# Gated delta rule on one core: GpSimd masks the decay before the rows' scales are known

## The chip, the cores and the metric

The kernel runs on one core of a Trainium2 chip, as one program with one launch. The metric is the device time of an execution in microseconds, the median of three runs. The profile is one execution that the hardware profiler recorded; its times count from the start of its span.

## The reference, cut to what matters

Two blocks run one after the other on 256 frames of width 1024 in float32. The first mixes two branches, a gated delta rule (8 heads of 64) and a sparse attention with an indexer, and then a mixture of experts. The second has a gated linear recurrence, an attention with forgetting and a dense feed-forward part. The change lies in the delta rule of the first block. It works in chunks of 64 frames; what it needs before its scan over the chunks is this (cut):

```python
G = jnp.cumsum(gc, axis=-1)
incl = idx[:, None] >= idx[None, :]
strict = idx[:, None] > idx[None, :]
decay = jnp.exp(jnp.where(incl, G[..., :, None] - G[..., None, :], -jnp.inf))
kk = jnp.einsum("bhnid,bhnjd->bhnij", kc, kc)
a_mat = jnp.where(strict, bc[..., :, None] * kk * decay, 0.0) + jnp.eye(CHUNK)
sol = lax.linalg.triangular_solve(a_mat, rhs, left_side=True, lower=True, unit_diagonal=True)
qk = jnp.einsum("bhnid,bhnjd->bhnij", qc, kc) * decay
k_dec = kc * jnp.exp(G[..., -1:] - G)[..., None]
```

The keys and queries are normalised first, so each row of the products also gets a factor of 1/norm. The decay, 64x64 for each of 8 heads and 4 chunks, is masked once strictly (for the triangular matrix) and once inclusively (for qk).

## The kernel before

Dense products (`tm`, L318, with tokens as rows; `fm`, L359, with features as rows) run in float32 split in two parts: a weight chunk `raw` comes by DMA from SP's queue, ACT rounds it to `whi` (L298), DVE subtracts to get `wlo` (L301), and TensorE adds three products (L333, L334, L335 in `tm`; L374, L375 or L379 to L381 in `fm`). Each of these tiles has four buffers. An accumulator `acc` in PSUM has to be emptied before its next use.

The branches are written as generators and drained piece by piece by `stream`; a scheduler at compile time then fixes the order in which each engine's queue takes its instructions. An engine takes its queue strictly in that order. So an edit in one place can give other orders for some hundreds of instructions on all engines.

The function `delta` (L583) runs, for each half `t` of 128 frames: the squares and norms of the queries and keys (`rk[t]` by the root iterations L179 to L199), the running log decay `R` (L629) and its product L632, the exponential `dec` (L634, ACT), the column `wk` of it (L644) and the scaled keys `kd` (L646, DVE), `br2` (L654), then four GpSimd products of 128x512 that give the masked and scaled decays `dl` and `di` (L658 to L663), and the products of keys and queries (L671, L672), which DVE multiplies with them to `LT` and `QK` (L673, L674). After both halves DVE scales keys and queries (L678, L679). From `LT` then follows, for both halves at once, a chain: `E` (L691 on ACT, L692 on DVE), `F`, `Lr`, `Ti`, fifteen pairs of small DVE instructions (L703, L705) that invert the 16x16 diagonal blocks, then L712 to L717, `DT` (L720) and `DD` (L724, ACT), the TensorE groups L737 with DVE's `X` (L741) between them, and the scan over the chunks (L774 to L803).

Beside it TensorE has the dense products of the same block to do: the third part of the convolution, four column groups `z_group` of the indexer (`zI`, two groups of 292 columns) and of the attention (`zB`, two groups of 384 columns), later the gate product with 512 columns (`sz`), then the wide `fm` products of the mixing gates (L374). The indexer's scores (L926) and the attention's logits (L955) lie between them. For each `z_group` ACT copies the two accumulators to `zI` or `zB` (L820).

Of the kernel before, what the change touches and what calls it, by code (L numbers as in the profile page):

```python
# [14 lines left out]
ALU = mybir.AluOpType  # L15
# [56 lines left out]
def body(ctx, tc, I, out, dbg=None):  # L72
    nc = tc.nc
    V, A, G, T, SY = nc.vector, nc.scalar, nc.gpsimd, nc.tensor, nc.sync
# [11 lines left out]
    def nm(s):  # L86
        cnt[0] += 1
        return f"{s}{cnt[0]}"
# [23 lines left out]
    def b2(shape, dt=F32, n="c"):  # L112
        return sp.tile(shape, dt, tag="b2" + st[0], name=nm(n), bufs=NB2[st[0]])
# [4 lines left out]
    def tiny(shape, dt=F32, n="t"):  # L118
        n_el = int(np.prod(shape[1:]))
        if n_el > 64:  # L120
            return sp.tile(shape, dt, tag="t128", name=nm(n), bufs=4)
        tag, bufs = ("t16", N16) if n_el <= 16 else ("t64", N64)
        return sp.tile(shape, dt, tag=tag + st[0], name=nm(n), bufs=bufs[st[0]])
# [12 lines left out]
    def sm():  # L136
        return pss.tile([128, 512], F32, tag="sm" + st[0], name=nm("sm"), bufs=NSM[st[0]])
# [12 lines left out]
    def C(k):  # L150
        o, n = COFF[k]
        return cst[:, o:o + n]
# [18 lines left out]
    def rsqrt(v, shape):  # L171
        return rsqrts([v], shape)[0]
# [404 lines left out]
    def hv(ap):  # L577

        return ap.rearrange("p (b q) -> p q b", q=2)
# [3 lines left out]
    def delta():  # L583
# [14 lines left out]
        rk, rki, kd, vs = [], [], [], []  # L598
# [3 lines left out]
        for t in range(2):  # L602
            ts_ = slice(t * 128, (t + 1) * 128)
            tk = []
            for src in (qT, kT):
                ps = sm()
                for b in range(4):
                    T.transpose(ps[:, b * 128:(b + 1) * 128], src[:, b, ts_], ident)
                tk.append(ps)
                junk = b2([128, 8, 64], n="sq")  # L610
                A.activation(junk.rearrange("p h d -> p (h d)"), ps, AF.Square)
                ss = tiny([128, 8])
                V.tensor_reduce(ss, junk, axis=AX.X, op=ALU.add)
                if src is qT:
                    oe = tiny([128, 8])
                    V.tensor_scalar(oe, ss, 64 * EPS, 256 * EPS * EPS, op0=ALU.mult, op1=ALU.add)
                    oeps.append(oe)
                else:
                    vv = tiny([128, 8])
                    V.tensor_scalar(vv, ss, 4 * EPS, None, op0=ALU.add)  # L620
                    r = rsqrt(vv, [128, 8])
                    ri = tiny([128, 8])
                    V.scalar_tensor_tensor(ri, vv, 0.5, r, op0=ALU.mult, op1=ALU.mult)
                    rk.append(r)
                    rki.append(ri)
            yield

            R = b2([128, 2, 4, 64], n="R")
            V.tensor_tensor(R, hv(gg[:, t])[:, :, :, None].to_broadcast([128, 2, 4, 64]),  # L629
                            C("inc")[:, None, None].to_broadcast([128, 2, 4, 64]), op=ALU.mult)  # L630
            pe = sm()
            T.matmul(pe, C("v64"), R.rearrange("p q b i -> p (q b i)"), start=True, stop=True)  # L632
            dec = b2([128, 2, 4, 64], n="dec")
            A.activation(dec.rearrange("p q b i -> p (q b i)"), pe, AF.Exp)  # L634
            pg = sm()
            gx = b2([128, 8, 64], n="gx")
            V.tensor_copy(gx, gg[:, t, :, None].to_broadcast([128, 8, 64]))
            for b in range(4):
                T.matmul(pg[:, b * 128:(b + 1) * 128], gx[:, 2 * b:2 * b + 2].rearrange("p h d -> p (h d)"), C("u64"),
                         start=True, stop=True)  # L640
            A.activation(eG[:, :, ts_], pg.rearrange("p (b t) -> p b t", b=4), AF.Exp)

            wk = tiny([128, 2, 4])
            V.tensor_tensor(wk, hv(rk[t]), dec[:, :, :, 63], op=ALU.mult)  # L644
            k_ = b2([128, 2, 4, 64], n="kd")
            V.tensor_tensor(k_, tk[1].rearrange("p (b q d) -> p q b d", q=2, d=64),  # L646
                            wk[:, :, :, None].to_broadcast([128, 2, 4, 64]), op=ALU.mult)
            kd.append(k_)
            yield

            br = tiny([128, 8])
            V.tensor_tensor(br, bet[:, t], rk[t], op=ALU.mult)
            br2 = tiny([128, 8])
            V.tensor_tensor(br2, br, rk[t], op=ALU.mult)  # L654
            oeps[t] = (oeps[t], br)
            dl = b2([128, 2, 4, 64], n="dl")
            di = b2([128, 2, 4, 64], n="di")
            G.tensor_tensor(dl, hv(br2)[:, :, :, None].to_broadcast([128, 2, 4, 64]),  # L658
                            C("str")[:, None, None].to_broadcast([128, 2, 4, 64]), op=ALU.mult)
            G.tensor_tensor(di, hv(rk[t])[:, :, :, None].to_broadcast([128, 2, 4, 64]),  # L660
                            C("inc")[:, None, None].to_broadcast([128, 2, 4, 64]), op=ALU.mult)
            G.tensor_tensor(dl, dl, dec, op=ALU.mult)
            G.tensor_tensor(di, di, dec, op=ALU.mult)  # L663
            for q in range(2):
                pk = sm()
                p4 = pk.rearrange("p (a b i) -> p a b i", a=2, b=4)
                for c in range(2):
                    cs = slice(t * 128 + c * 64, t * 128 + c * 64 + 64)
                    rw = slice(q * 64, q * 64 + 64)
                    for b in range(4):  # L670
                        T.matmul(p4[c * 64:c * 64 + 64, 0, b], kT[rw, b, cs], kT[rw, b, cs], start=True, stop=True)  # L671
                        T.matmul(p4[c * 64:c * 64 + 64, 1, b], kT[rw, b, cs], qT[rw, b, cs], start=True, stop=True)  # L672
                V.tensor_tensor(LT[:, t, q], p4[:, 0], dl[:, q], op=ALU.mult)  # L673
                V.tensor_tensor(QK[:, t, q], p4[:, 1], di[:, q], op=ALU.mult)  # L674
            yield
# [84 lines left out]
        for n in range(4):  # L760
            t, c = divmod(n, 2)
# [46 lines left out]
            yield  # L808

    dl_ = delta()  # L810
    stream("a", dl_)
    conv(2, vT)
# [1005 lines left out]
```

## Time and profile before

| | |
|---|---|
| median of three runs | 876.07 us (874.96 to 876.17) |
| time of the profiled execution | 880.68 us |
| span of the profiled execution | 878.9 us |
| mean granted TensorE clock | 0.981 |
| TensorE busy | 831.4 us, 95% of the span |
| VectorE (DVE) busy | 600.0 us, 68% |
| ScalarE (ACT) busy | 419.0 us, 48% |
| GpSimd (POOL) busy | 60.0 us, 7% |

Busy shares are means over stages with different limits. The profiled execution's own time stands 4.6 us above the median of the runs and 1.8 us above its span, so a time worked out from rows of the trace is on the trace's scale and has to be brought to that of the runs.

### The profile page before, as it was taken

What the parts mean: (1) busy time and instruction counts of PE and PEld (TensorE: products, weight loads), DVE (VectorE), ACT (ScalarE), POOL (GpSimd) and SP (SyncE); (2) the same over time, 40 slices, a digit from 0 to 9 for tenths busy, and PEclk for the clock granted to TensorE, in tenths of its full rate; (3) what the DMA queues carried; (4) which work ended last, traced back from release to release, by engine and by line L of the source; (5) the groups of instructions that cost most, each with busy time, mean ns of one, the idle gap of its engine ahead of it and who ended that gap; (6) DMA issues with size and microseconds to landing.
All of it is one profiled execution on the core that took longest, in us unless ns stands there. A gap on an engine that the chain in (4) does not pass through costs nothing.

```text
span 878.9 us, 14638 instructions
## 1 busy us (share of the span) xinstructions
PE 831.4 (95%) x5565; PEld 696.1 (79%) x5565; DVE 600.0 (68%) x1303; ACT 419.0 (48%) x743; POOL 60.0 (7%) x74
## 2 busy tenths in 40 slices
PE   4998899999998999999797998999999999999997
PEld 4997878788887766655797985889888888888876
DVE  5977996797777342415769789656886666674565
ACT  4754544366554011013664544665566556663443
POOL 5022030000000000000106103000000000000000
PEclk9999999799998999999899999999999999999999
DMA  8732561253678899966362573355665666675641
GB/s 232 205 87 73 173 195 50 66 173 114 221 272 300 293 385 348 385 212 207 130 185 72 141 218 110 91 168 189 211 197 150 188 191 186 180 212 198 193 158 48
DMA packets 107721, 162.81 MB, mean 185 GB/s; under 512 B 7272, under 2 KB 73584, under 8 KB 107648
## 3 DMA queue, kind: packets, MB, share of 16 engines
q1 hardware_dynamic: 107008, 161.71, 57.9%
q8 instruction: 45, 0.74, 0.3%
q0 software_dynamic: 640, 0.13, 0.2%
q14 instruction: 28, 0.23, 0.1%
HBM read 159.71 MB, written 2.11 MB: 184 GB/s over the span
## 4 chain that ended last, share of the span: by engine, by line
PE 43%; DVE 6%; issue 2%; ACT 1%; POOL 0%; DVEq 0%; POOLq 0%; ACTq 0%
PE acc L374 13%; PE acc L375 6%; PE acc L333 5%; PE acc L334 5%; PE acc L335 5%; PE acc L380 1%; PE acc L381 1%; PE acc L379 1%; PE sm L272 1%; DVE wlo L301 1%; PE sm L1662 1%; PE sm L1566 1%; PE sm L1690 1%; DVE ST L1567 0%; PE sm L1682 0%
## 5 line engine op out<-in xcount | busy, mean ns | idle before, releaser
L301 DVE TENSOR_TENSOR wlo<-raw,whi 128x1024 fp32r<-128x1024 f32 (+4 forms) x203 | 241.1, 1190 | 93.3 <-ACT whi L298 90.0
L298 ACT ACTIVATE whi<-raw 128x1024 fp32r<-128x1024 f32 (+4 forms) x203 | 207.0, 1022 | 149.9 <-PE acc L335 53.4
L374 PE MATMUL acc<-hx,whi 128*128 128x512 f32 x608 | 214.1, 403 | 0.9 <-DVE hx L255 0.9
L375 PE MATMUL acc<-hx,wlo 128*128 128x256 f32 x608 | 161.6, 286 | 0.0
L333 PE MATMUL acc<-whi,hx 128*128 128x512 f32 (+4 forms) x376 | 139.6, 371 | 7.3 <-ACT zI L820 3.7
L335 PE MATMUL acc<-whi,hx 128*128 128x512 f32 (+4 forms) x376 | 138.4, 368 | 0.0
L334 PE MATMUL acc<-wlo,hx 128*128 128x512 f32 (+4 forms) x376 | 138.4, 368 | 0.1
L374 PEld LDWEIGHTS acc<-hx,whi 128*128 128x128 f32 x608 | 110.5, 190 | 23.0 <-issue 1.3
L375 PEld LDWEIGHTS acc<-hx,wlo 128*128 128x128 f32 x608 | 115.9, 191 | 8.0 <-issue 0.7
L333 PEld LDWEIGHTS acc<-whi,hx 128*128 128x128 f32 x376 | 71.1, 189 | 18.4 <-ACT zI L820 4.5
L380 PE MATMUL acc<-hx,whi 128*128 128x256 f32 x288 | 81.6, 284 | 1.4 <-DVE hx L258 1.4
L379 PE MATMUL acc<-hx,whi 128*128 128x256 f32 x288 | 81.1, 284 | 1.5 <-ACT hx L257 1.5
L381 PE MATMUL acc<-hx,wlo 128*128 128x256 f32 x288 | 81.9, 285 | 0.0
L335 PEld LDWEIGHTS acc<-whi,hx 128*128 128x128 f32 x376 | 71.1, 189 | 9.8 <-issue 0.5
L334 PEld LDWEIGHTS acc<-wlo,hx 128*128 128x128 f32 x376 | 71.2, 189 | 9.3 <-DVE wlo L301 0.5
L1253 PE MATMUL acc<-we,xg 128*64 128x256 f32 x512 | 64.8, 383 | 0.0
L379 PEld LDWEIGHTS acc<-hx,whi 128*128 128x128 f32 x288 | 54.8, 192 | 2.4 <-ACT hx L257 2.0
L380 PEld LDWEIGHTS acc<-hx,whi 128*128 128x128 f32 x288 | 55.2, 191 | 2.0 <-DVE hx L258 1.8
L381 PEld LDWEIGHTS acc<-hx,wlo 128*128 128x128 f32 x288 | 55.2, 192 | 0.4 <-issue 0.2
L1253 PEld LDWEIGHTS acc<-we,xg 128*64 128x64 f32 x512 | 37.8, 137 | 21.3 <-issue 5.4
L386 DVE TENSOR_TENSOR both<-both,acc 128x256 f32<-128x256 f32 x76 | 31.6, 416 | 20.9 <-ACT both L385 20.0
L385 ACT ACTIVATE both<-acc 128x256 f32<-128x256 f32 x76 | 28.8, 380 | 33.6 <-PE acc L374 33.5
(456 smaller groups left out, 1126.1 us busy)
## 6 DMA issues: line engine op xcount, KB each, us to landing
raw<-in_w_in SPq DMA_DIRECT2D x64, 512.0 KB, 3.8
we<-in_w_exp_gate SPq DMA_DIRECT2D x32, 512.0 KB, 7.6
we<-in_w_exp_up SPq DMA_DIRECT2D x32, 512.0 KB, 7.9
wd<-in_w_exp_down SPq DMA_DIRECT2D x64, 256.0 KB, 6.5
raw<-in_w_ffn_gate SPq DMA_DIRECT2D x22, 512.0 KB, 3.8
raw<-in_w_ffn_up SPq DMA_DIRECT2D x22, 512.0 KB, 3.9
raw<-in_w_ffn_down SPq DMA_DIRECT2D x22, 512.0 KB, 4.4
raw<-in_w_out SPq DMA_DIRECT2D x16, 512.0 KB, 4.3
```

The source lines that it names most:

```text
L298: A.activation(hi[:, :n], raw[:, :n], AF.Copy)
L301: (eng or V).tensor_tensor(lo[:, :n], raw[:, :n], hi[:, :n].bitcast(F32), op=ALU.subtract)
L333: T.matmul(ps[t][:, c], ht.hi(kk, a, b), wh[:, k, c], start=kk == 0, stop=False)
L334: T.matmul(ps[t][:, c], ht.hi(kk, a, b), wl[:, k, c], start=False, stop=False)
L335: T.matmul(ps[t][:, c], ht.lo(kk, a, b), wh[:, k, c], start=False, stop=kk == K - 1)
L374: two = [lambda: T.matmul(ps[f], wh[:, k, c], ht.both(kk), start=kk == 0, stop=kk == K - 1), lambda: T.matmul(ps[f][:, :S], wl[:, k, c], h ...
L375: lambda: T.matmul(ps[f][:, :S], wl[:, k, c], ht.hi(kk), start=False, stop=False)]
L379: T.matmul(ps[f][:, :S], wh[:, k, c], ht.hi(kk), start=kk == 0, stop=False)
L380: T.matmul(ps[f][:, :S], wh[:, k, c], ht.lo(kk), start=False, stop=False)
L381: T.matmul(ps[f][:, :S], wl[:, k, c], ht.hi(kk), start=False, stop=kk == K - 1)
L386: V.tensor_tensor(both, both, ps[f][:, :S], op=ALU.add)
L1253: T.matmul(ph[64 * q:64 * q + 64, i * 256:(i + 1) * 256], xgs[pr // 2][k // 4][:, k % 4, e * 64:(e + 1) * 64], ups[ex][k // 4, i][:, k % 4 ...
```

## The change

For each half, GpSimd now multiplies the decay with the strict mask into `dl` and with the inclusive mask in place (`di` is `dec`'s own tile) right behind the exponential. `wk` reads its column after that (column 63 of the inclusive mask is one in all its rows, so the value is the same). Once the rows' scales are there, one GpSimd product puts `br2` into `dl` and one DVE product puts `rk[t]` into `di`. Line numbers on the left of the diff's second part are not those of the kernel before: L658 to L663 before answer to L637, L639, L661, L662 after, and `wk` is L649 instead of L644.

```diff
             dec = b2([128, 2, 4, 64], n="dec")
             A.activation(dec.rearrange("p q b i -> p (q b i)"), pe, AF.Exp)
+
+            dl = b2([128, 2, 4, 64], n="dl")
+            G.tensor_tensor(dl, dec, C("str")[:, None, None].to_broadcast([128, 2, 4, 64]), op=ALU.mult)
+            di = dec
+            G.tensor_tensor(di, dec, C("inc")[:, None, None].to_broadcast([128, 2, 4, 64]), op=ALU.mult)
             pg = sm()
             gx = b2([128, 8, 64], n="gx")
...
             V.tensor_tensor(br2, br, rk[t], op=ALU.mult)
             oeps[t] = (oeps[t], br)
-            dl = b2([128, 2, 4, 64], n="dl")
-            di = b2([128, 2, 4, 64], n="di")
-            G.tensor_tensor(dl, hv(br2)[:, :, :, None].to_broadcast([128, 2, 4, 64]),
-                            C("str")[:, None, None].to_broadcast([128, 2, 4, 64]), op=ALU.mult)
-            G.tensor_tensor(di, hv(rk[t])[:, :, :, None].to_broadcast([128, 2, 4, 64]),
-                            C("inc")[:, None, None].to_broadcast([128, 2, 4, 64]), op=ALU.mult)
-            G.tensor_tensor(dl, dl, dec, op=ALU.mult)
-            G.tensor_tensor(di, di, dec, op=ALU.mult)
+            G.tensor_tensor(dl, dl, hv(br2)[:, :, :, None].to_broadcast([128, 2, 4, 64]), op=ALU.mult)
+            V.tensor_tensor(di, di, hv(rk[t])[:, :, :, None].to_broadcast([128, 2, 4, 64]), op=ALU.mult)
             for q in range(2):
```

Three places show how the orders move. The first is DVE's queue at the second half (t = 1), from `wk` on. Before:

```order
169 L644 TENSOR_TENSOR t_795<-ry_767,dec_785 128x8
170 L652 TENSOR_TENSOR t_799<-t_588,ry_767 128x8
171 L646 TENSOR_TENSOR kd_797<-sm_752,t_795 128x512
172 L654 TENSOR_TENSOR t_801<-t_799,ry_767 128x8
173 L678 TENSOR_TENSOR qkvT_250<-qkvT_250,eG_634 128x1024
174 L679 TENSOR_TENSOR qkvT_249<-qkvT_249,eG_634 128x1024
175 L673 TENSOR_TENSOR LT_632<-sm_809,dl_803 128x256
176 L674 TENSOR_TENSOR QK_633<-sm_809,di_804 128x256
```

The same place of the changed kernel (`dec_784` is the tile that GpSimd masks in place; `wlo_1605` is the last weight part of the second `zI` group):

```order
168 L649 TENSOR_TENSOR t_797<-ry_766,dec_784 128x8
169 L657 TENSOR_TENSOR t_801<-t_588,ry_766 128x8
170 L651 TENSOR_TENSOR kd_799<-sm_751,t_797 128x512
171 L659 TENSOR_TENSOR t_803<-t_801,ry_766 128x8
172 L662 TENSOR_TENSOR dec_784<-dec_784,ry_766 128x512
173 L677 TENSOR_TENSOR qkvT_250<-qkvT_250,eG_634 128x1024
174 L672 TENSOR_TENSOR LT_632<-sm_807,dl_786 128x256
175 L673 TENSOR_TENSOR QK_633<-sm_807,dec_784 128x256
176 L672 TENSOR_TENSOR LT_632<-sm_826,dl_786 128x256
178 L678 TENSOR_TENSOR qkvT_249<-qkvT_249,eG_634 128x1024
179 L691 SCALAR_TENSOR_TENSOR E_847<-LT_632,cst,E_847 128x16x16 x2
180 L301 TENSOR_TENSOR wlo_1605<-raw_1601,whi_1603 128x584
```

A new 128x512 product (L662) stands in the queue, the second scaling of the queries has moved behind `LT` and `QK`, and `wlo_1605`, which before was taken at row 157, ahead of the root iterations, now stands behind `E`.

The second place is DVE's queue where the weight parts of the second `zB` group are made, within and behind the chain of small instructions. Before (`wlo_1705` is that group's first chunk):

```order
210 L703 TENSOR_TENSOR t_893<-Lr_856,Ti_858 128x48
211 L301 TENSOR_TENSOR wlo_1705<-raw_1701,whi_1703 128x768
212 L705 TENSOR_TENSOR Ti_858<-Ti_858,t_893 128x4x12
213 L301 TENSOR_TENSOR wlo_1723<-raw_1719,whi_1721 128x768
214 L703 TENSOR_TENSOR t_896<-Lr_856,Ti_858 128x39
215 L301 TENSOR_TENSOR wlo_1741<-raw_1737,whi_1739 128x768
```

The changed kernel, where the same first chunk is `wlo_1703`:

```order
226 L716 TENSOR_TENSOR y_909<-Y_907 128x16x16
227 L714 STREAM_TRANSPOSE Y_914<-Z_912 128x512
228 L719 TENSOR_TENSOR DT_904<-y_909,cst 128x1024
229 L716 TENSOR_TENSOR y_916<-Y_914 128x16x16
230 L301 TENSOR_TENSOR wlo_1703<-raw_1699,whi_1701 128x768
231 L572 SCALAR_TENSOR_TENSOR qkvT_251<-ct_1176,cy_1171 128x256
232 L301 TENSOR_TENSOR wlo_1721<-raw_1717,whi_1719 128x768
233 L301 TENSOR_TENSOR wlo_1739<-raw_1735,whi_1737 128x768
```

The chunk has moved from the twelfth pair of the loop to behind the whole chain up to `DT` and `y`.

The third place is TensorE's queue around the first group of L737 (the first use of `DD`). Before, it comes when the second `zB` group is all but done:

```order
582 L335 MATMUL acc_1700<-whi_1757,hx_134 128x384
583 L333 MATMUL acc_1700<-whi_1757,hx_134 128x384
584 L737 MATMUL sm_924<-DD_905,LT_632 64x64 x16
585 L334 MATMUL acc_1700<-wlo_1759,hx_134 128x384
586 L335 MATMUL acc_1700<-whi_1757,hx_134 128x384
587 L333 MATMUL acc_2190<-whi_2194,hx_131 128x512
```

In the changed kernel it comes behind the sixth matmul of that group:

```order
537 L335 MATMUL acc_1622<-whi_1679,hx_134 128x384
538 L333 MATMUL acc_1697<-whi_1701,hx_131 128x384
539 L334 MATMUL acc_1697<-wlo_1703,hx_131 128x384
543 L335 MATMUL acc_1697<-whi_1701,hx_131 128x384
544 L736 MATMUL sm_922<-DD_903,LT_632 64x64 x16
545 L333 MATMUL acc_1698<-whi_1701,hx_131 128x384
```

Forty matmuls of 128x384 thus stand behind L737's first group instead of ahead of it. Later in the queue, between the first L737 and the first wide `fm` matmul (L374), before has 2 of 128x384 and 48 of 128x512 among the small products, all 48 ahead of the last logits (L955). The changed kernel has 42 of 128x384 and 20 of 128x512 there, and the other 28 of 128x512 in one piece between L955 and L374.

## Rows read from the trace of the kernel before

**Rows 1.** The cores' spans and mean granted clock.

```profile
core 0: 878.9 us, clock 0.981
```

**Rows 2.** Windows of 20 us: length, busy time of each engine (instructions), clock, DMA.

```profile
80.00:100.00 20.00, 15.61 (x92) 14.69 (x92) 16.71 (x52) 7.88 (x12) 2.45 (x2) 1.00 0.36 112
100.00:120.00 20.00, 17.67 (x285) 15.06 (x284) 19.90 (x44) 13.79 (x22) 1.97 (x2) 1.00 0.49 143
...
140.00:160.00 20.00, 20.00 (x192) 15.80 (x192) 13.04 (x32) 7.93 (x18) 0.00 (x0) 0.83 0.17 54
160.00:180.00 20.00, 20.00 (x96) 16.70 (x95) 15.52 (x45) 9.12 (x15) 0.00 (x0) 0.83 0.38 106
```

**Rows 3.** TensorE's waits from 74 to 130 us: total, times, longest.

```profile
PE acc L333 <- ACT zI L820: 3.7, 2, 3.2
PE acc L333 <- ACT zB L820: 1.7, 3, 0.6
PE sm L737 <- DVE X L741: 1.0, 1, 1.0
```

**Rows 4.** Timeline of GpSimd: start, duration, instruction (idle before, releaser).

```profile
76.06 1.90 POOL L658 TENSOR_TENSOR dl<-t,cst 128x512 f32<-128x512 f32 x1 [11.19 <-DVE t L654]
...
79.91 1.28 POOL L662 TENSOR_TENSOR dl<-dl,dec 128x512 f32<-128x512 f32 x1
```

**Rows 5.** Timeline of DVE around the second half's masks.

```profile
71.10 0.76 DVE L301 TENSOR_TENSOR wlo<-raw,whi 128x584 fp32r<-128x584 f32 x1
...
74.95 0.17 DVE L644 TENSOR_TENSOR t<-ry,dec 128x8 f32<-128x8 f32 x1
...
75.15 0.69 DVE L646 TENSOR_TENSOR kd<-sm,t 128x512 f32<-128x512 f32 x1
...
75.83 1.22 DVE L678 TENSOR_TENSOR qkvT<-qkvT,eG 128x1024 f32<-128x1024 f32 x1
76.97 2.07 DVE L679 TENSOR_TENSOR qkvT<-qkvT,eG 128x1024 f32<-128x1024 f32 x1
81.23 0.42 DVE L673 TENSOR_TENSOR LT<-sm,dl 128x256 f32<-128x256 f32 x1 [2.19 <-POOL dl L662]
```

**Rows 6.** Timeline of ACT in the same stretch.

```profile
71.33 0.60 ACT L634 ACTIVATE dec<-sm 128x512 f32<-128x512 f32 x1 [0.79 <-PE sm L632]
...
83.33 1.22 ACT L691 ACTIVATE E<-LT,cst 128x256 f32<-128x256 f32 x2 [3.81 <-DVE LT L673]
...
85.83 0.40 ACT L820 ACTIVATE zI<-acc 128x292 f32<-128x292 f32 x1
```

**Rows 7.** Timeline of TensorE, the last accumulator of `zI`, the first of `zB`.

```profile
79.58 0.40 PE L333 MATMUL acc<-whi,hx 128*128 128x292 f32 x1 [0.50 <-ACT zI L820]
...
82.75 0.29 PE L335 MATMUL acc<-whi,hx 128*128 128x292 f32 x1
86.28 0.44 PE L333 MATMUL acc<-whi,hx 128*128 128x384 f32 x1 [3.23 <-ACT zI L820]
...
91.31 0.44 PE L333 MATMUL acc<-whi,hx 128*128 128x384 f32 x1 [0.58 <-ACT zB L820]
```

**Rows 8.** DVE: one of the four `wlo` in the loop; the chain's last step.

```profile
94.68 0.95 DVE L301 TENSOR_TENSOR wlo<-raw,whi 128x768 fp32r<-128x768 f32 x1
...
103.81 0.60 DVE L717 TENSOR_TENSOR y<-Y 128x256 f32<-128x256 f32 x1
```

**Rows 9.** TensorE at the first group of L737 and at the gates' first `fm` matmul.

```profile
106.20 1.15 PE L737 MATMUL sm<-DD,LT 64*64 64x64 f32 x32 [0.78 <-ACT DD L724]
...
161.65 0.79 PE L374 MATMUL acc<-hx,whi 128*128 128x512 f32 x1
```

**Rows 10.** Windows of a chosen length, columns as in the windows above.

```profile
129.00:134.00 5.00, 5.00 (x74) 4.14 (x72) 3.50 (x7) 0.85 (x2) 1.69 (x3) 1.00 0.36 138
...
144.30:155.30 11.00, 11.00 (x118) 8.90 (x117) 5.47 (x12) 3.68 (x8) 0.00 (x0) 0.91 0.27 87
155.30:166.00 10.70, 10.70 (x37) 7.83 (x37) 8.25 (x26) 2.97 (x6) 0.00 (x0) 0.50 0.06 8
```

## The prediction

> **What bounds the kernel now.** I looked first at the cores' row [rows 1]: one core, 878.9 us, and a granted clock of 0.981, so a little of the time is spent at the lower of TensorE's two levels. TensorE is busy for 95% of the span. A change that touches only small work on GpSimd and DVE can therefore save only where TensorE stands still or runs slowly. The windows of 20 us give the first place [rows 2]: 4.4 us idle in 80 to 100, 2.3 us in 100 to 120. The list of its waits names them [rows 3]: 3.7 us for ACT's copy `zI`, of which 3.2 in one piece, 1.7 us for copies of `zB`, 1.0 for `X`.
>
> The long one isn't ACT's slowness. The copy started at 85.83 because ACT had `E` ahead of it in its queue, and `E` started at 83.33 after 3.81 us in which ACT waited for `LT` [rows 6]. `LT` started at 81.23, after DVE had waited 2.19 us for GpSimd's `dl` [rows 5]. GpSimd had started its four products at 76.06, when `br2` was there, and its third ended at 81.19 [rows 4]. So the chain that stops TensorE until 86.28 [rows 7] is GpSimd, `LT`, `E`, `zI`, and the change works on its first link.
>
> The second place is the clock. It is 0.83 in the windows from 140 to 160 and from 160 to 180 [rows 2], with TensorE busy for all 40 us. The work lost is 40 x (1 - 0.83) = 6.8 us, and since TensorE never waits there, all of it is on the path. In 155.3 to 166 the clock is 0.50, the lower level, throughout; the 11 us before have 0.91, and consist of small products (64x64, and 64 rows deep) with no 128x512 matmul among them until the last [rows 10]. Idling isn't what came before this drop, and the 3.23 us of idling at 83 to 86 left the clock at 1.00 [rows 2, 7].
>
> **What is removed and added, at the second half.** `dec` ends at 71.33 + 0.60 = 71.9 now [rows 6]. The changed queues have less ahead of it on TensorE and ACT, and I put its end at 70.0. GpSimd's two masks follow. Such a mask stands nowhere in the trace; the nearest rows are 1.28 us for a plain product with DVE quiet and 1.90 beside DVE's 128x1024 products [rows 4]. So the two end at 72.6 to 73.8. `wk` stood at 74.95 [rows 5], behind the root iterations; without the `wlo` that have left its queue there (0.76 us at 71.10, and a larger one) DVE gets to it at about 72.6, so it waits 0 to 1.2 us for the mask in place. Behind it stand `kd`, `br2` and all else of DVE, but this wait is paid out of a gain of over 2 us. Then come `kd` with 0.69 us, the new DVE product, a 128x512 like `kd`, 0.69 [rows 5], the scaling of the keys, 1.22, and GpSimd's one product beside it, 1.28 to 1.90. `LT` starts at 76.3 to 77.7, middle 77.0; `E` on ACT at about 78.0 instead of 83.33. The same edits at the first half lie ahead of a stretch in which DVE waits for work, and I cost them at nothing (0.69 us of DVE if that cover were gone).
>
> GpSimd and DVE disturb each other in these rows: L658 took 1.90 beside the scalings, and L679 took 2.07 against 1.22 of its like L678 [rows 4, 5]. The Trainium skill ("SBUF — State Buffer", section "Who interferes with whom") says why: a DVE instruction with two SBUF inputs and a GpSimd instruction that reads SBUF take a shared port in turn, and the one that comes second blocks. By that rule each mask next to a DVE product is at the far end of the range above, `LT` comes at 77.7, and the sum is 0.7 us worse than with the middle.
>
> **Where the stall goes.** `E` is out of the way when `zI` is to be copied, so the 3.2 us go. What is late next is on DVE, by the changed order. *First*, `wlo_1605`, the last weight part of the second `zI` group, was made at 71.10 [rows 5]; now it stands behind `LT` and `QK` (four at 0.4, from 77.0 to 78.5), the scaling of the queries (1.2) and `E` (0.6), and is there 0.76 later, at about 81. TensorE gets to that group's first accumulator at about 76.5 and wants the last chunk after 18 matmuls of (82.75 - 79.58) / 23 = 0.14 us [rows 7], at 79.1: a wait of 1.8 us. With the copies of the accumulators, 0.5 to 0.6 each as before, `zB` starts at about 86.0, against 86.28 [rows 7]. So of the 3.2 us only 0.3 is kept here.
>
> *Second*, `wlo_1703`, the first chunk of the second `zB` group. Its like was made at 94.68, inside the loop of small instructions [rows 8]. Now it stands behind the whole chain to the second L717. That chain took from 83.33 to 104.41 before [rows 6, 8], 21.1 us, with seven `wlo` of 768 in it (0.95 us each, some 0.9 net). After, it starts at 78.0 and has four of these and the 0.76 of `wlo_1605`: 78.0 + 21.1 - 3 x 0.9 + 0.8 = 97.2, and with the part of the queries' scaling that `E` doesn't cover some 98.0. Then `wlo_1703` is there at 98.95. One accumulator of a `zB` group takes 91.31 - 86.28 = 5.0 us with its copy [rows 7], so TensorE wants it at 86.0 + 10.1 = 96.1: a wait of 2.8 us. L737's first group comes six matmuls later, at (5.0 - 0.6) / 24 = 0.18 us each: at 100.0. Before, it came at 106.20 [rows 9], and forty matmuls, 7.2 us, no longer stand ahead of it: like for like 99.0. So TensorE is 1.0 us behind here.
>
> *Third*, two further `wlo` of 0.95 stand ahead of the first `X`, and others ahead of the next ones; I put TensorE's waits for `X` at 2.9 us in three pieces (bounds 0 and 4), against 1.0 before [rows 3]: 1.9 more. One copy of 0.6 falls into these waits; I take off half of it, 0.3. Sum: 1.0 + 1.9 - 0.3 = **2.6 us slower**, with bounds of 0.5 (masks at 1.28, no waits for `X`) and 4.5 (masks at 1.90, waits of 4). DVE is the reason: it was busy for 19.90 of the 20 us from 100 to 120 already [rows 2], and the new order makes TensorE meet that.
>
> **The clock.** The filler between the small products changes: twenty 128x512 and 42 of 128x384 instead of 48 and 2, in another spread. In the changed queue I count no piece of small products alone above some 5 us, where the one ahead of the drop had 11, and 28 matmuls of 128x512 follow right behind L955. Before, the five microseconds from 129 to 134, mostly such products, stayed at 1.00 [rows 10]. So I expect that the clock stays at full, which gives the 6.8 us back. The Trainium skill ("TensorE: Matmul & The Clock Gate", Part 1) says that "activity releases the throttle"; no row here tells whether the new mixture does. The gates' first matmul was at 161.65 [rows 9], in the middle of the drop; behind it I see nothing to give back or take away. Expert weights are loaded in another order on SP's queue, which I cost at nothing: the gates' products stand ahead of their use and hide them, and if they don't, it costs some us.
>
> **Sum.** -6.8 + 2.6 = -4.2 us. The profiled execution took 880.68 us, 1.8 more than its span and 4.6 more than the median of 876.07; a difference carries over: 876.07 - 4.2 = about 872.0 us.
>
> **Rivals.**
> - *The drop comes back* as long as before: the small products are the same in number. Then only the new DVE waits are left: 876.07 + 2.6 = 878.7, slower. By the middle of the waits it decides from 2.6 / 0.5 = 5.2 us fewer at the lower level on: a drop that shrinks by less leaves the kernel slower. For it speaks that nothing of the small products is gone, against it the window from 129 to 134. 0.22.
> - *It comes, but for half as long*, since dense work follows sooner: 3.4 given back, 876.07 - 0.8 = 875.3, no change to be measured. 0.15.
> - *The gain is as simple as it looks*: the new places of the `wlo` cost nothing, the 3.2 us are kept and the clock too: 876.07 - 10.0 = 866. Against it stand the order and DVE's full window. 0.08.
> - *The change doesn't advance `LT`*: `wk` waits so long for the mask in place that `br2` comes no earlier. `LT` would have to start at 81.2 still, for which each mask would have to take 4 us; no row comes near. No change, 876. 0.03.
> - My forecast, 0.52, with its own range of 870 to 874.
>
> **Numbers.** A measurement tells about 0.2%, 1.75 us, from no change. Faster: the forecast and the simple gain, 0.60. Same: no advance and most of the half drop, 0.16. Slower: the drop and the rest, 0.24. The range is 868.5 to 879.5: it leaves out the simple gain and what lies beyond the bounds.
>
> **What would show it.** Right: `LT` of the second half at 76 to 78; no 3 us wait for `zI`; new waits of TensorE for `wlo` near 79 and 96; the first L737 near 100; a clock of 1.00 from 140 to 180; the gates' first matmul at 160 to 162. Wrong: a clock of 0.50 there, or where it wasn't before; no wait for `wlo`; `LT` after 79; TensorE idle for expert weights.

## The result and the profile after

The change makes the kernel slower. The first comparison has 882.62 us (881.88 to 883.33, 4 runs) against 876.12 us before, a ratio of 1.0058 (95% interval 1.0034 to 1.0081). A second one, with 10 and 28 runs, has 879.55 against 876.92: 1.0032 (1.0011 to 1.0052). The sign is the same in both; that the sizes differ has to do with the clock, as the section on the prediction shows. The forecast was 872.0, with a range of 868.5 to 879.5.

The profiled execution after took 881.88 us, with a span of 880.1. These are the windows of 20 us after, which answer to [rows 2]:

```profile
80.00:100.00 20.00, 15.94 (x87) 14.80 (x85) 17.59 (x54) 7.49 (x11) 0.00 (x0) 0.91 0.36 99
100.00:120.00 20.00, 17.54 (x323) 15.62 (x322) 18.42 (x39) 8.49 (x16) 0.00 (x0) 0.91 0.44 134
140.00:160.00 20.00, 19.16 (x166) 14.24 (x165) 15.46 (x42) 8.21 (x17) 2.52 (x2) 1.00 0.25 79
160.00:180.00 20.00, 19.30 (x105) 16.47 (x104) 19.82 (x59) 12.64 (x19) 0.00 (x0) 1.00 0.51 139
```

The clock is at 1.00 from 140 to 180, as forecast, but it is 0.91 twice from 80 to 120, where it was 1.00. TensorE's waits from 74 to 130 us after, for [rows 3]:

```profile
PE acc L334 <- DVE wlo L301: 4.4, 2, 2.5
PE acc L333 <- ACT zI L819: 1.5, 3, 0.5
PE acc L333 <- ACT zB L819: 1.2, 2, 0.6
```

The 3.2 us for `zI` are gone, and 4.4 us for two weight parts stand in their place. Now what the change was made for. GpSimd's timeline after, for both halves (some rows left out at the marks):

```profile
54.95 1.72 POOL L637 TENSOR_TENSOR dl<-dec,cst 128x512 f32<-128x512 f32 x1 [0.84 <-ACT dec L634]
59.44 0.09 POOL L563 MEMSET zc<- 128x3 f32 x1 [2.77 <-DVE ry L199]
59.50 1.26 POOL L639 TENSOR_TENSOR dec<-dec,cst 128x512 f32<-128x512 f32 x1
...
71.96 1.28 POOL L637 TENSOR_TENSOR dl<-dec,cst 128x512 f32<-128x512 f32 x1 [7.77 <-ACT dec L634]
73.31 1.97 POOL L639 TENSOR_TENSOR dec<-dec,cst 128x512 f32<-128x512 f32 x1
76.88 1.43 POOL L661 TENSOR_TENSOR dl<-dl,t 128x512 f32<-128x512 f32 x1 [1.59 <-DVE t L659]
```

And DVE's beside it (some of its rows):

```profile
55.44 1.27 DVE L620 TENSOR_SCALAR t<-t 128x8 f32<-128x8 f32 x1
...
59.63 1.16 DVE L197 TENSOR_TENSOR ra<-ra,rh 128x8 f32<-128x8 f32 x1
...
72.74 1.42 DVE L301 TENSOR_TENSOR wlo<-raw,whi 128x876 fp32r<-128x876 f32 x1 [1.09 <-ACT whi L298]
74.09 1.23 DVE L196 TENSOR_TENSOR ra<-ry 128x8 f32<-128x8 f32 x1
...
75.83 0.17 DVE L649 TENSOR_TENSOR t<-ry,dec 128x8 f32<-128x8 f32 x1
...
77.32 2.08 DVE L677 TENSOR_TENSOR qkvT<-qkvT,eG 128x1024 f32<-128x1024 f32 x1
79.31 0.41 DVE L672 TENSOR_TENSOR LT<-sm,dl 128x256 f32<-128x256 f32 x1
...
82.93 0.75 DVE L301 TENSOR_TENSOR wlo<-raw,whi 128x584 fp32r<-128x584 f32 x1
```

Three instructions on 8 numbers per partition, which take 0.17 us elsewhere, took 1.16 to 1.27. Each started while a GpSimd product was under way and ended within 0.1 us of it: 55.44 + 1.27 = 56.71 against 54.95 + 1.72 = 56.67; 60.79 against 60.76; 75.32 against 75.28. The same goes for the scaling of the keys (2.08 us instead of the 1.2 of its like): it ends at 79.40, 1.1 us behind the end of GpSimd's L661 at 78.31. The fourth early mask (L637 at 71.96) met a weight part: L301 with 876 columns took 1.42 us at 72.74, against 1.07 for its like at 49.77. So three of the four early masks fall on DVE's root iterations and the step ahead of them, a chain of tiny instructions, and hold them up by about a microsecond each. The column `wk` (L649) has no wait for the mask left: it starts at 75.83, behind the iterations, and the mask ended at 75.28.

TensorE's timeline after, at the places of [rows 7, 9]:

```profile
52.98 0.67 PE L632 MATMUL sm<-R,cst 128*128 128x512 f32 x1
...
83.74 0.40 PE L334 MATMUL acc<-wlo,hx 128*128 128x292 f32 x1 [2.47 <-DVE wlo L301]
...
90.70 0.45 PE L333 MATMUL acc<-whi,hx 128*128 128x384 f32 x1 [0.50 <-ACT zI L819]
...
103.11 0.69 PE L334 MATMUL acc<-wlo,hx 128*128 128x384 f32 x1 [1.88 <-DVE wlo L301]
...
105.01 0.48 PE L736 MATMUL sm<-DD,LT 64*64 64x64 f32 x4
...
164.28 0.39 PE L374 MATMUL acc<-hx,whi 128*128 128x512 f32 x1
```

`zB` starts at 90.70, where it was 86.28 [rows 7] and 86.0 was forecast. The first group with `DD` (L737 before, L736 here) comes at 105.01 instead of 100.0, and the gates' first matmul at 164.28 instead of 160 to 162.

### The profile page after: what moved, and what is told of

Its sections match the earlier page's. It is cut to its first block, busy times and chain, and to the rows that moved or that the text cites. A ratio compares the mean times of both kernels' runs of the same rounds, so it can differ in the third digit from the quotient of the medians.

```text
span 880.1 us, 14637 instructions
## 1 busy us (share of the span) xinstructions
PE 830.9 (94%) x5565; PEld 696.1 (79%) x5565; DVE 604.6 (69%) x1305; ACT 417.9 (47%) x741; POOL 59.1 (7%) x72
## 4 chain that ended last, share of the span: by engine, by line
PE 43%; DVE 6%; issue 2%; ACT 1%; POOL 0%; DVEq 0%; POOLq 0%; ACTq 0%
PE acc L374 13%; PE acc L375 6%; PE acc L333 5%; PE acc L334 5%; PE acc L335 5%; PE acc L380 1%; PE acc L381 1%; PE acc L379 1%; PE sm L272 1%; DVE wlo L301 1%; PE sm L1661 1%; PE sm L1565 1%; PE sm L1689 1%; DVE ST L1566 0%; PE sm L1681 0%
## 5 line engine op out<-in xcount | busy, mean ns | idle before, releaser
L301 DVE TENSOR_TENSOR wlo<-raw,whi 128x1024 fp32r<-128x1024 f32 (+4 forms) x203 | 239.7, 1184 | 95.3 <-ACT whi L298 92.2
L298 ACT ACTIVATE whi<-raw 128x1024 fp32r<-128x1024 f32 (+4 forms) x203 | 207.2, 1023 | 151.2 <-PE acc L335 62.8
L374 PE MATMUL acc<-hx,whi 128*128 128x512 f32 x608 | 212.9, 400 | 1.6 <-DVE hx L255 0.9
L374 PEld LDWEIGHTS acc<-hx,whi 128*128 128x128 f32 x608 | 109.8, 188 | 23.7 <-issue 1.3
```

Source lines behind the costliest of these rows:

```text
L298: A.activation(hi[:, :n], raw[:, :n], AF.Copy)
L301: (eng or V).tensor_tensor(lo[:, :n], raw[:, :n], hi[:, :n].bitcast(F32), op=ALU.subtract)
L374: two = [lambda: T.matmul(ps[f], wh[:, k, c], ht.both(kk), start=kk == 0, stop=kk == K - 1), lambda: T.matmul(ps[f][:, :S], wl[:, k, c], h ...
```

## The experiments

Two theories were tested. **A, the order**: the weight parts behind the chain make TensorE wait, and the clock falls behind these waits. **B, GpSimd beside DVE**: the early masks hold up DVE's small instructions, and with them everything behind. Each comparison has its own runs of the kernel before on the same chip; their medians are 878.54 (first four), 876.92 (next four) and 877.46 (last four). The last column is a stretch of the profiled execution that the start-up doesn't touch: from the first product with `R` to the first `zB` matmul, in us. The line numbers in the text are those of each run's own kernel.

| kernel | median us | lowest to highest | ratio to before (95%) | R to zB |
|---|---|---|---|---|
| before again | 879.06 | 875.6 to 880.7 | 1.0007 (0.9990 to 1.0025) | 33.75 |
| own tile | 880.89 | 878.5 to 883.7 | 1.0032 (1.0014 to 1.0050) | 39.45 |
| all on DVE | 877.87 | 876.0 to 878.9 | 0.9993 (0.9978 to 1.0008) | 33.08 |
| last on DVE | 876.24 | 875.3 to 877.6 | 0.9984 (0.9969 to 1.0000) | 34.56 |
| change again | 879.55 | 878.2 to 884.0 | 1.0032 (1.0011 to 1.0052) | 37.70 |
| dummy masks | 883.75 | 878.0 to 885.7 | 1.0072 (1.0047 to 1.0097) | 37.42 |
| early masks only | 879.81 | 877.0 to 883.1 | 1.0031 (1.0016 to 1.0046) | 37.00 |
| DVE, free accumulators | 871.63 | 869.9 to 878.3 | 0.9956 (0.9933 to 0.9979) | 28.76 |
| dummy fills | 876.54 | 874.9 to 880.8 | 0.9989 (0.9968 to 1.0010) | 33.08 |
| before, free accumulators | 872.18 | 869.3 to 875.1 | 0.9945 (0.9923 to 0.9967) | 28.69 |
| last on DVE, free accumulators | 877.26 | 874.0 to 883.3 | 1.0011 (0.9985 to 1.0037) | 28.61 |
| no strict mask, free accumulators | 869.61 | 866.9 to 870.9 | 0.9903 (0.9873 to 0.9933) | 28.78 |

For the profiles shown ahead, the stretch is 86.28 - 52.52 = 33.76 before and 90.70 - 52.98 = 37.72 after. Drops of the clock inside the stretch are part of these figures. By the mean clock of the stretch they take some 1.8 us in the change, change again, dummy masks and early masks only, 5.1 in own tile, 0.3 in before again and nothing in the others. The start of L632 before:

```profile
52.52 0.67 PE L632 MATMUL sm<-R,cst 128*128 128x512 f32 x1
```

One estimate more helps to read the table. An execution's span times its mean granted clock is about the time that it would take if the lost clock were given back (it takes off too much where TensorE stands still during a drop). Its medians are 861.3 to 861.7 us in the three sets of before, 866.3 and 865.9 in the two of the change, 864.2 for own tile, 863.3 for all on DVE, 864.5 for the dummy masks and 862.4 for the dummy fills. By it the change loses some 4.4 us besides the clock.

**Before again** (no edit).

> The kernel before, unchanged, for its clock. If the drop to the lower clock that the profiled execution showed from 153 to 167 us belongs to every execution, the runs have a mean clock of about 0.981 and this profile shows 0.83 in the windows 140 to 160 and 160 to 180 again. If it belongs to some executions only (the profiled one took 880.7 us, the median run 876.1), the runs near 876 have a mean clock of 0.985 to 0.99 and a profile of such a run shows no drop or a shorter one there, and the 6.8 us that the prediction counted as a gain were not to be had.

The second case as to the place of the drop; as to its size the answer is mixed. Of the 12 runs the three below 877 us have mean clocks of 0.984 to 0.987, those above 880 have 0.980 or 0.981, and the median run, 879.06, lies nearer to the latter. The drop isn't tied to a place. Two windows of this profile (880.27 us):

```profile
80.00:100.00 20.00, 15.60 (x76) 14.73 (x76) 15.13 (x46) 7.89 (x12) 2.46 (x2) 0.83 0.28 80
140.00:160.00 20.00, 20.00 (x211) 15.73 (x208) 13.71 (x32) 8.95 (x19) 0.00 (x0) 1.00 0.17 54
```

The lower clock comes at 80 to 100, around the end of the same wait (3.24 us here) that left it at 1.00 in the other profile [rows 2, 7], and not at 140 to 180. The unchanged kernel thus spreads over 5.1 us here, and its mean clocks of 0.980 to 0.987 account for that size (0.007 x 878 = 6.1 us). No profile was taken of a run near 876; that it has little of either drop is inferred from its mean clock.

**Own tile.** The inclusive mask is not made in place.

```diff
-            di = dec
+            di = b2([128, 2, 4, 64], n="di")
```

> The change with one thing undone: the inclusive mask goes into a tile of its own, so that the column for the keys' scale reads the unmasked decay. GpSimd still masks early. Its order is like that of the kernel before in the stretch from the first key product to the sparse attention: 94 matmuls of 128x384 stand ahead of the first group on the inverse, and the weight parts stand within the small instructions. Theory A (the order: weight parts behind the chain, and the clock falls after the waits they bring) expects 871 to 877 us and no waits of TensorE for a weight part near 81 and 101 us. Theory B (GpSimd's early masks hold up DVE's root iterations, about 1 us for each mask, and this carries through) expects 880 to 884 us, as with the whole change.

Theory A's number was missed: no wait for a weight part, an order like before, and still 880.9. GpSimd's two masks, now one right behind the other, meet L620 and L179 (1.29 and 1.26 us instead of 0.17), and its third product meets the copy `gx` (1.27 instead of 0.42). In this order `gx` stands behind the whole root chain, so the three holds (1.12, 1.09 and 0.85 us) all reach it. TensorE waits 2.30 us for it and then runs at a lower clock, 0.53 from 63 to 74 us:

```profile
PE sm L644 <- DVE gx L642: 2.3, 1, 2.3
```

Without the 5.1 us of the drop the stretch would be 34.3 us, near the 33.75 of before. So in this profile the loss up to `zB` comes mostly by way of the clock.

**All on DVE.**

```diff
-            G.tensor_tensor(dl, dec, C("str")[:, None, None].to_broadcast([128, 2, 4, 64]), op=ALU.mult)
+            V.tensor_tensor(dl, dec, C("str")[:, None, None].to_broadcast([128, 2, 4, 64]), op=ALU.mult)
...
-            G.tensor_tensor(di, dec, C("inc")[:, None, None].to_broadcast([128, 2, 4, 64]), op=ALU.mult)
+            V.tensor_tensor(di, dec, C("inc")[:, None, None].to_broadcast([128, 2, 4, 64]), op=ALU.mult)
...
-            G.tensor_tensor(dl, dl, hv(br2)[:, :, :, None].to_broadcast([128, 2, 4, 64]), op=ALU.mult)
+            V.tensor_tensor(dl, dl, hv(br2)[:, :, :, None].to_broadcast([128, 2, 4, 64]), op=ALU.mult)
```

> The change with its three GpSimd products on DVE too (two masks and one scale for each half, 0.69 us each), so no GpSimd work beside DVE in this stretch. The order stays that of the change: 54 matmuls of 128x384 ahead of the first group on the inverse, weight parts behind the chain. Theory A (the order) expects the waits for weight parts of about 2 us each again and 880 to 884 us. Theory B (GpSimd beside DVE) expects the small DVE instructions back at 0.17 us, the matrix L of the second half 1 to 2 us earlier than with the change, and 875 to 878 us.

Theory B: the median lies 4.7 us below the first comparison's 882.6 and 1.7 below the second's 879.6, and against the runs of before that belong to each, the ratio is 0.9993 where the change had 1.0058 and 1.0032. This is so though DVE has 2 us more work for each half (three products of 0.69). `LT` of the second half starts here:

```profile
75.20 0.42 DVE L672 TENSOR_TENSOR LT<-sm,dl 128x256 f32<-128x256 f32 x1
```

That is 23.17 us behind the first product with `R` (52.03), where the change needs 79.31 - 52.98 = 26.33: 3.2 us ahead. What A said is seen too, but smaller: the waits for weight parts stay (0.92 and 1.99 us). The estimate without the clock puts this kernel at 863.3 us, 1.7 above before. So something remains that the median hides behind somewhat higher clocks (0.984 to 0.987).

**Last on DVE**, the second part of the change alone.

```diff
-            G.tensor_tensor(di, di, dec, op=ALU.mult)
+            V.tensor_tensor(di, di, dec, op=ALU.mult)
```

> Only the second part of the change, in the kernel before: the last of GpSimd's four products behind the rows' scale goes to DVE, nothing is masked early. Order like before (96 of 128x384 ahead of the first group on the inverse). Theory A expects 873 to 877 us, with the 3.2 us wait for the indexer's copy still there or little shorter. Theory B has nothing that would slow it down and expects the same; more than 879 would speak against both.

This is within the expectation, with a ratio just at no change. The wait for `zI` is 3.07 us as before.

**Change again** (no edit).

> The changed kernel, unchanged, for as many executions as the kernel before now has (its runs lie from 874.9 to 881.4, with clocks of 0.988 to 0.980). Expected 881 to 884 us with clocks of 0.980 to 0.986; against the whole set of runs of before, median 878.5, that is 3 to 5 us slower, where the first comparison had 6.5. If its runs reach down to 877 as well, the difference is mostly the luck of the clock.

Lower than forecast: most runs lie at 878 to 880 with clocks of 0.985 to 0.988. Its profile repeats the holds (L620 1.27, L197 1.16, L196 1.23, L677 2.07) and the stretch of 37.7 us to two hundredths. The executions differ in their mean clocks.

**Dummy masks.** All on DVE, and two unread GpSimd products for each half.

```diff
             A.activation(eG[:, :, ts_], pg.rearrange("p (b t) -> p b t", b=4), AF.Exp)
+            for m in ("str", "inc"):
+                jk = sp.tile([128, 2, 4, 64], F32, tag="junk", name=nm("junk"), bufs=1)
+                G.tensor_tensor(jk, eG[:, :, ts_].rearrange("p b (q i) -> p q b i", q=2), C(m)[:, None, None].to_broadcast([128, 2, 4, 64]), op=ALU.mult)
```

> The kernel with all of the change's products on DVE (877.9 us) and two GpSimd products of 128x512 for each half added, right behind the exponential eG, with a result that nobody reads; the queues of TensorE, DVE and ACT are the same, row by row. If GpSimd only costs by being beside DVE (theory B), small DVE instructions of the root iterations take about 1.2 us again, L of the second half comes 1 to 3 us later, and the run takes 880 to 883 us. If the change's loss is its waits and its data (the mask in place, wk behind it), the dummies cost nothing: 877 to 878.5 us.

This decides. Nothing waits for the dummies, the other three engines take the same instructions in the same order, and the kernel takes 883.75 instead of 877.87 us (1.0072 and 0.9993 of before, in their own comparisons). GpSimd and the root iterations of the second half in its timeline:

```profile
72.00 2.67 POOL L649 TENSOR_TENSOR junk<-eG,cst 128x512 f32<-128x512 f32 x2 [11.06 <-ACT eG L646]
```

```profile
71.86 0.17 DVE L196 TENSOR_TENSOR ra<-ry 128x8 f32<-128x8 f32 x1
72.06 1.26 DVE L197 TENSOR_TENSOR ra<-ra,rh 128x8 f32<-128x8 f32 x1
73.35 0.17 DVE L199 SCALAR_TENSOR_TENSOR ry<-ra,ry 128x8 f32<-128x8 f32 x1
73.55 1.15 DVE L623 SCALAR_TENSOR_TENSOR t<-t,ry 128x8 f32<-128x8 f32 x1
```

One hold for each GpSimd product, of its whole length. TensorE pays by way of the weight parts: its longest wait for one is 2.87 us, 0.92 without the dummies, and the clock is 0.91 and 0.83 from 80 to 120. The stretch is 37.42 us, that of the change to 0.3 us, against 33.08 without the dummies; some 1.8 of these 4.3 us are a drop of the clock inside it. Of the 5.9 us in the median, too, the larger part goes with lower mean clocks (median 0.981 against 0.9855): without the clock the two kernels are at 864.5 and 863.3 us.

**Early masks only**, both scales on GpSimd.

```diff
-            V.tensor_tensor(di, di, hv(rk[t])[:, :, :, None].to_broadcast([128, 2, 4, 64]), op=ALU.mult)
+            G.tensor_tensor(di, di, hv(rk[t])[:, :, :, None].to_broadcast([128, 2, 4, 64]), op=ALU.mult)
```

> Only the first part of the change: the early masks, with both scales on GpSimd (the last product is not on DVE). Theory B expects it slow like the change, 880 to 884 us, with DVE's small instructions of 1.2 us beside the masks, and L of the second half about 1 us later than with the change, since two products instead of one follow the rows' scale. If it takes 878 or less, the slow part of the change is the product on DVE and not the early masks.

Slow like the change, if just below the expected 880; so the loss belongs to the early masks and not to DVE's product. `LT` starts at 76.27, 24.75 us behind the first product with `R`, and not later than with the change (26.33) as I expected: the order differs in its neighbourhood.

**DVE, free accumulators.** All on DVE, and in `conv`:

```diff
-            A.activation(y, ps, AF.Copy, scale=cw[3])
+            A.activation(y, zc[:, 3:], AF.Copy, scale=cw[3])
```

> A try at a version that beats both: all products of the change on DVE, and the convolution's scaled copy is read from zc instead of from the accumulator, so that the third part's two accumulators are free at 65 us instead of 106 and the column groups can alternate between two pairs. Six copies of about 0.55 us each that TensorE waits for should go, 3 us, and the waits for weight parts should move; against that, more of the dense work is used up before the small products, and TensorE may wait among these. Expected 872 to 877 us; over 878 would say that the used-up filler costs more than the copies.

871.63, faster than both kernels. The profiled execution took 875.10 us, and its clock is 0.83 from 140 to 180 again, as in the first profile of before. The waits for copies and weight parts are gone; what is left between 40 and 140:

```profile
PE sm L736 <- ACT DD L723: 2.0, 1, 2.0
PE sm L784 <- DVE vs L755: 1.2, 1, 1.2
PE sm L608 <- DVE qkvT L572: 0.2, 1, 0.2
```

**Dummy fills**: the dummies write and read nothing.

```diff
+            for m in range(2):
+                G.memset(gx, 0.0)
             A.activation(eG[:, :, ts_], pg.rearrange("p (b t) -> p b t", b=4), AF.Exp)
```

> As the kernel with dummy masks (883.8 us, against 877.9 without them), but the dummies are GpSimd fills: two of 128x512 for each half, behind the reads of gx, which write and read nothing; the queues of the other engines are the same again. If it is GpSimd's reading beside DVE that holds DVE up, the small DVE instructions stay at 0.17 us and the time at 876 to 879 us. If any GpSimd work of this size beside DVE does, they go to 0.7 to 1.2 us and the time to 880 to 884.

No cost: 876.54, the stretch again 33.08. DVE's group of L197 in 50 to 82 us, with the dummy masks and then with the fills:

```profile
L197 DVE TENSOR_TENSOR ra<-ra,rh 128x8 f32<-128x8 f32 x6 | 3.2, 531 | 0.1
```

```profile
L197 DVE TENSOR_TENSOR ra<-ra,rh 128x8 f32<-128x8 f32 x6 | 1.0, 164 | 0.1
```

The fills are shorter (two take 1.11 us, two dummy masks 2.67), so they cover less of DVE's chain; but at 57.5 and 70.5 they lie beside it, and no instruction is held. Of the pair at 70.45, four steps of the iterations (L199, L196, L197, L199, from 70.83 to 71.43) start under it and take 0.16 to 0.17 us each:

```profile
70.45 1.11 POOL L647 MEMSET gx<- 128x512 f32 x2 [11.80 <-PE sm L644]
```

A GpSimd product of the length of a fill wasn't tried.

**Before, free accumulators** (the edit in `conv` alone).

> The kernel before with the accumulators freed early alone (the scaled copy of the convolution is read from zc). It tells apart what in the 871.6 us of the last try belongs to this and what to the products on DVE. If the freed accumulators bring all of it, 870 to 873 us; if the earlier L by the products on DVE is needed, the chain from GpSimd by way of L still stops TensorE where the filler is used up, and it takes 874 to 878 us.

872.18: nearly all of the gain of the last try is this. The wait for `zI` is down to 1.65 us.

**Last on DVE, free accumulators** (both single edits).

> The freed accumulators with the second part of the change alone (the last product behind the rows' scale on DVE, no early masks). Between the kernel before with freed accumulators and the one with all products on DVE: 871 to 876 us. If it is as fast as the latter (871.6), early masks are of no use even on DVE.

Outside the expectation, 877.26, slower than either edit alone. Its filler of 128x512 is used up before the small products (31 of 48 stand ahead of L737's first group), and TensorE waits there (2.10, 1.02, 0.94 us). That can't be the whole reason: the last kernel, 5 us faster, has 30 of 48 ahead of that group and waits of 1.96 and 0.89 us. What differs most is the mean clock, a median of 0.981 (down to 0.978) against 0.986, which makes some 4.4 of the 5.1 us; why it is lower isn't shown. Two edits that are harmless or good alone weren't additive here.

**No strict mask, free accumulators.** All on DVE; `dl` is the inclusively masked decay times `br2`.

```diff
-            V.tensor_tensor(dl, dec, C("str")[:, None, None].to_broadcast([128, 2, 4, 64]), op=ALU.mult)
...
-            V.tensor_tensor(dl, dl, hv(br2)[:, :, :, None].to_broadcast([128, 2, 4, 64]), op=ALU.mult)
+            V.tensor_tensor(dl, dec, hv(br2)[:, :, :, None].to_broadcast([128, 2, 4, 64]), op=ALU.mult)
```

> The freed accumulators, all products on DVE, and the strict mask left out: the entries of L on and above the diagonal are not read by the steps behind it, so one product of 0.69 us for each half goes, and L of the second half comes some 0.7 to 1.4 us earlier. Expected 869 to 874 us; as fast as with the strict mask (871.6) if the chain behind L, and not its start, decides.

869.61, the fastest of all, 0.97% under before (0.67 to 1.27). TensorE's waits in 40 to 140:

```profile
PE acc L334 <- DVE wlo L301: 0.6, 1, 0.6
PE sm L790 <- DVE vn L785: 0.3, 1, 0.3
PE sm L608 <- DVE qkvT L572: 0.2, 1, 0.2
PE sm L783 <- DVE vs L754: 0.2, 1, 0.2
```

That the shorter work on DVE and not just another order brings the last 2 us isn't shown: the two differ in both, and the intervals touch. The earlier `LT` that I expected didn't come: it starts at 79.52, 24.3 us behind the first product with `R`, against 22.8 with the strict mask.

## Why the prediction was wrong, by its own steps

- *What bounds the kernel now*: right. The chain GpSimd, `LT`, `E`, `zI` stopped TensorE; with `LT` earlier by 81.23 - 79.31 = 1.9 us, and TensorE itself later at that place, this wait went. One part of the way was left out: between `E` and the copy ACT also had two roundings of weight chunks (L298, from 84.36 to 85.92).
- *What is removed and added, the second half*: **this step failed.** I put `LT` at 77.0 and `E` at 78.0; they started at 79.31 and 80.42, and an `LT` after 79 was among my own signs of being wrong. `dec` came at 71.28 + 0.60, no earlier than before (70.0 was a guess from the order):

```profile
71.28 0.60 ACT L634 ACTIVATE dec<-sm 128x512 f32<-128x512 f32 x1 [2.16 <-PE sm L632]
...
80.42 0.78 ACT L690 ACTIVATE E<-LT,cst 128x256 f32<-128x256 f32 x1 [1.29 <-DVE LT L672]
```

Above all I used the rule of the Trainium skill ("SBUF — State Buffer", section "Who interferes with whom") for one side only, for how long GpSimd's products take, and costed the masks as work beside DVE. The rule says that whichever comes second blocks. Here GpSimd was first and DVE second, five times: 1.10, 0.99, 1.06, 0.87 and 0.35 us (L620, L197, L196, L677 and the weight part at 72.74, each less its usual duration), 4.4 us over both halves. The trace of before had the pattern on show, L679 with 2.07 [rows 5], and I read it as GpSimd's disturbance, not as a price that the moved products take with them.
- *The first half "at nothing"*: failed by the same reason. The hold on L620 delays `gx`, which stands right behind it, and TensorE waited 0.95 us at 57 us ahead of the product that reads `gx` (the profile names L183, the step next to it); the in-place mask stood behind a fill that waited for DVE until 59.44.
- *Where the stall goes*: the mechanism was right, both weight parts made TensorE wait. The first was mis-sized at 1.8 (2.47, since `E` was late; 0.92 with all on DVE), the second at 2.8 (1.88). The waits for `X`, put at 2.9, didn't come at all. `zB` started at 90.7 and not at 86.0. L736 at 105.01 is 5.0 us behind the forecast: 2.4 of it is the late `E`, and in the chain behind it DVE waited another 0.70 and 0.86 us for `whi`. My lower bound of 0.5 doesn't follow from its own terms either: masks at 1.28 take 0.7 off the 1.0, and no wait for `X` is 1.0 less than before, which makes about -0.7.
- *The clock*: the drop from 140 to 180 went, as forecast, but **the -6.8 us weren't there to be had**. **This step failed too.** I took the drop of one execution as a property of the kernel, tied to the small products, and let the difference carry over to a median that stood 4.6 us below it. The extra runs show clocks of 0.988 to 0.978 for the unchanged kernel and the drop at another place. After the change the two interruptions at 81 to 84 and 100 to 103 each came with one: the windows of 80 to 120 have 20 x 0.09 twice, 3.6 us lost.

Both terms can be set against the runs. Among executions of the same mean clock, all comparisons taken together, before has a median of 875.1 us at 0.987 (18 runs) and the change 878.8 and 879.6; at 0.982 it is 878.9 (22 runs) against 883.3 and 883.5. So the waits and the order, put at 2.6, cost some 4 us at an equal clock. The clock, put at -6.8, went from a median of 0.984 to 0.986 in the second comparison, which is worth about -0.002 x 878 = -1.8 us. The two make up the 2.6 us measured there; in the first, the change's four runs had a median clock of 0.9835 and show 6.5.

The sum with the measured terms, from `R` to `zB`, change against before: TensorE's waits were 0.95 + 2.47 + 4 x 0.50 = 5.4 us (before 0.50 + 3.23 = 3.7), and the clock lost 1.7 us at 84 to 90 after (2 us times 0.02, 0.50 and 0.34, from the windows below). That is 3.4 of the 3.96 us by which the stretch grew; 0.5 are not assigned. The second wait for a weight part, 1.88 us, lies behind this stretch.

```profile
84.00:86.00 2.00, 1.50 (x11) 1.26 (x11) 2.00 (x6) 0.41 (x1) 0.00 (x0) 0.98 0.48 136
86.00:88.00 2.00, 2.00 (x10) 2.00 (x10) 1.20 (x7) 0.77 (x1) 0.00 (x0) 0.50 0.79 224
88.00:90.00 2.00, 2.00 (x12) 1.96 (x11) 1.30 (x3) 0.65 (x2) 0.00 (x0) 0.66 0.12 40
```

The rival on the other side ("the drop comes back", 878.7) had the right sign and, with 878.7 - 876.07 = 2.6 us, the size of the second comparison. That is luck: it wasn't the old drop that came back, but held DVE instructions and new drops. "The change doesn't advance `LT`" was nearer to the mechanism, and I gave it 0.03, since I looked for masks of 4 us each instead of for DVE being stopped.

Shown by experiments: that GpSimd products which read, beside DVE, cost this kernel 4.3 us up to `zB` and 5.9 in the median even if nobody reads their result (dummy masks against all on DVE), drops of the clock included, and that fills, of less than half the length, don't. Only read from traces and mean clocks: how the loss splits into waits and clock. Argued and not tested by itself: the share of the order, some 1.7 us by the estimate for all on DVE. Open: why a drop follows a given wait in one execution and not in the next.

## What to carry to other kernels

Before work is moved to GpSimd "because it is idle", look at what DVE does in that time. Here GpSimd products of 1.26 to 1.97 us stopped a DVE instruction that came second for up to 1.1 us, and on a chain of tiny dependent instructions nearly every product cost one such stop. A profile is one execution: before a term of a forecast is taken from a drop of the clock, compare the profiled execution's time with the median, and if it stands above it by about that term, don't count on the term. A few runs are not enough for that median: three gave 876.07 here, and the later sets of 28 to 35 have 876.9 to 878.5. Look also for a buffer that is held too long: here an accumulator, freed by an edit of one operand, was worth 877.46 - 872.18 = 5.3 us, where the change, which was to make the producer earlier, brought a loss.

## What the hardware showed that I hadn't expected

A DVE instruction on 8 elements per partition took 1.15 to 1.29 us instead of 0.17 when it met a GpSimd product of 128x512, and ended with it. This held for forms with two inputs in SBUF (L196, L197, L623) and for scalar forms with one (L620, L179); a copy with one input, `gx` of 128x512 in own tile, took 1.27 instead of 0.42. The Trainium skill ("SBUF — State Buffer", section "Who interferes with whom") names both kinds, the latter by way of DVE's 2-port modes; no run here shows which mode L620 or the copy ran in. The same section of the Trainium skill says that GpSimd instructions that only write don't contend with two-input DVE instructions; the fills (0.164 us for L197) agree. The same kernel's executions spread from 873.9 to 883.0 us, and their mean clocks from 0.988 to 0.978 with them.
